# The shifted copies of the rotary embedding, issued on the ACT queue instead of the SP queue

## Chip, cores and metric

The kernel runs on one core of a Trainium2 chip. The metric is the device time of one execution in microseconds (us); lower is better. The engines are named as in the profile: PE does the matrix products, DVE, ACT and POOL work elementwise, and SP does no arithmetic: it issues DMA transfers. Each engine takes its instructions strictly in order, and so does each queue of DMA issues.

## What is computed

A two-layer encoder over 16 meta tokens and 512 tokens of width 2048. Layer 0 is attention with 16 query heads and 8 key heads of width 128; layer 1 is a gated linear attention. The change touches layer 0 alone, where every query and key head is normalised and rotated:

```python
def _rotate(x, ang):
    x1, x2 = jnp.split(x, 2, axis=-1)
    return jnp.concatenate([x1 * cos - x2 * sin, x2 * cos + x1 * sin], axis=-1)
...
q = apply_axial_rope(rmsnorm(q, q_norm), ang_row, ang_col)
k = apply_axial_rope(rmsnorm(k, k_norm), ang_row, ang_col)
...
p = softmax(q k^T / sqrt(128)); o = p v; y = (o * silu(gate)) @ w_out
```

A head is held with its 128 channels on the partitions and the 528 tokens along the free axis. The rotation mixes channels 0 to 31 with 32 to 63, and 64 to 95 with 96 to 127, so it needs a copy of the head in which these blocks of 32 partitions have changed places.

## The kernel before

Every float32 product is made of three matmuls on split operands (high by high, high by low, low by high): `uh` and `ul` are the normalised input, `whi` and `wlo` the weights. A unit of weights is 512 KB: SP loads it into `wraw` (two buffers, L151), ACT casts it to `whi` (L133), DVE takes the rest as `wlo` (L134), with three buffers of each.

Layer 0 runs over eight groups g of one key head and two query heads. While the attention of group g runs, `qkv(g + 1)` projects the next key head and the two next query heads, and `rope` rotates each: 24 rotations in all, three of them one right after the other at the start (group 0) and 21 spread over the groups. I call the three of a group K, Q1 and Q2. The steps of one rotation are these:

- ACT evacuates the two halves of the projection to `qw` (L293) and their squares to `sq` (L294);
- four DMAs, 32 partitions each, write the shifted copy `qs` from `qw` (L301); `qs` has one buffer;
- ACT and DVE split the squares into `sh` and `sl` (L133, L134), POOL multiplies `qw` by the cosines (L306, which overwrites what the four copies read) and `qs` by the sines (L307);
- PE sums the squares into `ssq` (L312, L313), DVE adds epsilon (L314), ACT makes the reciprocal root (L137, L138);
- DVE adds the two products (L316), multiplies by the root (L317), and ACT and DVE split the result into `qh`, `ql` or `kh`, `kl`.

Around them stand the steps of the attention: PE makes the scores `s` (L561 to L563), DVE their maximum `mx` (L566), ACT the exponentials `pn` (L569), DVE scales them (L570 to L572), PE transposes them to `pT` and, for the meta tokens, `pTm` (L579, L581), ACT copies these to `ph` and `pmt` (L583, L585), DVE takes the rests `pl` and the low part of `pmt` (L584, L586), and PE forms the output `o` (L599 to L602, ACT copies it at L603). `pT`, `pTm` and `ssq` share two PSUM buffers in turn, so a `pTm` can be written only when the last-but-one of these tiles has been read.

The code is written in one order, and the scheduler of the framework sets the order on each engine from priorities and its own estimate of durations. Weights have the higher priority: they are written to be issued up to 400 steps ahead.

Of the kernel before, what the change touches and what calls it, by code (L numbers as in the profile page):

```python
# [82 lines left out]
def hybrid_encoder(  # L83
# [5 lines left out]
    nc = tc.nc  # L89
# [42 lines left out]
    def split(hi, lo, src):  # L132
        A.copy(hi, src)  # L133
        V.tensor_tensor(lo, src, hi.bitcast(F32), op=ALU.subtract)  # L134

    def rsqrt_inplace(t):
        A.activation(t, t, AF.Ln)  # L137
        A.activation(t, t, AF.Exp, scale=-0.5)  # L138
# [158 lines left out]
    def rope(qw, sq, outs, ps_t):  # L297
        qs = wk.tile([P, T], F32, tag="qs", name="qs", bufs=1)
        for b in range(4):
            s = b ^ 1  # L300
            nc.sync.dma_start(out=qs[b * 32:b * 32 + 32, :], in_=qw[s * 32:s * 32 + 32, :])  # L301
        sh = wk.tile([P, T], F32R, tag="sh", name="sh", bufs=1)
        sl = wk.tile([P, T], F32R, tag="sl", name="sl", bufs=1)
        split(sh, sl, sq)
        f = sq
        G.tensor_tensor(qw, qw, cos, op=ALU.mult)  # L306
        G.tensor_tensor(qs, qs, sin, op=ALU.mult)  # L307

        def late():
            for a, b in HALVES:  # L310
                ps = ps_t.tile([P, 512], F32, tag="t", name="ssq")[:, :b - a]
                PE.matmul(ps, ones_r, sh[:, a:b], start=True, stop=False)  # L312
                PE.matmul(ps, ones_r, sl[:, a:b], start=False, stop=True)  # L313
                V.scalar_tensor_tensor(f[:, a:b], ps, 1.0 / P, erow[:, a:b], op0=ALU.mult, op1=ALU.add)  # L314
            rsqrt_inplace(f)
            V.tensor_tensor(qw, qw, qs, op=ALU.add)  # L316
            V.tensor_tensor(qw, qw, f, op=ALU.mult)  # L317
            for hi, lo, a, b in outs:
                split(hi, lo, qw[:, a:b])
        clk.after(3.7, late)  # L320
# [173 lines left out]
    for i in range(3):  # L494
        rope(*(taken(i) if i else head0), first_outs[i], ps_t)
        clk.flush()
# [44 lines left out]
    def qkv(g):  # L541
        qk, outs = qk_tiles()
        for i, c in enumerate((2048 + g * P, 2 * g * P, (2 * g + 1) * P)):
            qw, sq, evac = take(col(KN if i == 0 else QN))
            project(w_in0, c, HALVES, evac)
            rope(qw, sq, outs[i], ps_t)
        return qk, values(g)
# [811 lines left out]
```

## Time and profile before

| | |
|---|---|
| median of 3 runs | 1792.9 us (1791.56 to 1793.84) |
| the profiled execution | 1794.37 us, of which the span from first to last instruction is 1792.7 us |
| PE busy | 1766.4 us (99%) |
| DVE busy | 1036.8 us (58%) |
| ACT busy | 923.0 us (51%) |
| POOL busy | 199.1 us (11%) |
| the shifted copies | 96 DMAs of 66 KB, issued from 64.4 to 656.3 us |

The span is the time from the first to the last instruction. Issuing a DMA is not counted as busy time of an engine, but the queue of that engine stands while it lasts. In the rows of the profile an arrow `<-` behind a bracketed or listed time says how long the engine stood idle and whose result ended that.

### The profile page before, as it was taken

What the parts mean: (1) busy time and instruction counts of PE and PEld (TensorE: products, weight loads), DVE (VectorE), ACT (ScalarE), POOL (GpSimd) and SP (SyncE); (2) the same over time, 40 slices, a digit from 0 to 9 for tenths busy, and PEclk for the clock granted to TensorE, in tenths of its full rate; (3) what the DMA queues carried; (4) which work ended last, traced back from release to release, by engine and by line L of the source; (5) the groups of instructions that cost most, each with busy time, mean ns of one, the idle gap of its engine ahead of it and who ended that gap; (6) DMA issues with size and microseconds to landing.
All of it is one profiled execution on the core that took longest, in us unless ns stands there. A gap on an engine that the chain in (4) does not pass through costs nothing.

```text
span 1792.7 us, 31687 instructions
## 1 busy us (share of the span) xinstructions
PE 1766.4 (99%) x12711; PEld 1666.8 (93%) x12711; DVE 1036.8 (58%) x1807; ACT 923.0 (51%) x1875; POOL 199.1 (11%) x257
## 2 busy tenths in 40 slices
PE   8999999999999999999999999999999999999998
PEld 7899999999999999999999899988898989888886
DVE  4586555555656565632237887667685865764224
ACT  5665544454545454533238544477685765853221
POOL 3211111111111111111111101110000000000000
PEclk9999999999999999999999999999999999999999
DMA  8322232323232333343336444343242333344333
GB/s 260 119 61 83 84 89 84 89 83 90 83 89 82 91 105 94 121 131 91 96 92 205 120 128 132 93 135 96 83 113 82 103 95 88 92 151 176 94 95 129
DMA packets 263876, 193.93 MB, mean 108 GB/s; under 512 B 9356, under 2 KB 239440, under 8 KB 263200
## 3 DMA queue, kind: packets, MB, share of 16 engines
q1 hardware_dynamic: 254624, 162.52, 31.6%
q0 software_dynamic: 9104, 29.38, 4.7%
q8 instruction: 100, 1.64, 0.4%
q14 instruction: 48, 0.39, 0.1%
HBM read 160.88 MB, written 24.49 MB: 103 GB/s over the span
## 4 chain that ended last, share of the span: by engine, by line
PE 86%; DVE 5%; issue 3%; DMA 3%; ACT 2%; POOL 1%; SPq 0%; DVEq 0%; POOLq 0%; ACTq 0%
PE pp L156 18%; PE pp L158 18%; PE pp L157 18%; PE f L1271 2%; PE f L1269 2%; PE f L1270 2%; PE pp L233 2%; PE pp L235 2%; PE pp L234 2%; PE pT L579 2%; DMA wraw<-in_attn_w_in_dram 1%; PE s L561 1%; PE s L562 1%; PE s L563 1%; DVE wlo L134 1%
## 5 line engine op out<-in xcount | busy, mean ns | idle before, releaser
L156 PE MATMUL pp<-uh,whi 128*128 128x264 f32 (+1 forms) x2640 | 803.4, 304 | 0.8 <-ACT sq L294 0.4
L157 PE MATMUL pp<-ul,whi 128*128 128x264 f32 (+1 forms) x2640 | 793.9, 301 | 2.5 <-DVE ul L421 2.5
L158 PE MATMUL pp<-uh,wlo 128*128 128x264 f32 (+1 forms) x2640 | 794.0, 301 | 0.4 <-POOL wlo L360 0.3
L158 PEld LDWEIGHTS pp<-uh,wlo 128*128 128x128 f32 x2640 | 498.0, 189 | 17.5 <-POOL wlo L360 0.6
L156 PEld LDWEIGHTS pp<-uh,whi 128*128 128x128 f32 x2640 | 497.6, 189 | 17.4 <-ACT sq L294 0.5
L157 PEld LDWEIGHTS pp<-ul,whi 128*128 128x128 f32 x2640 | 498.2, 189 | 16.6 <-DVE ul L421 3.1
L134 DVE TENSOR_TENSOR wlo<-wraw,whi 128x1024 fp32r<-128x1024 f32 (+1 forms) x245 | 298.5, 1219 | 336.3 <-ACT whi L133 334.7
L133 ACT CAST whi<-wraw 128x1024 fp32r<-128x1024 f32 (+1 forms) x245 | 255.1, 1042 | 360.0 <-PE pp L157 197.5
L569 ACT ACTIVATE pn<-s,mx 128x528 f32<-128x528 f32 (+1 forms) x72 | 50.4, 700 | 105.6 <-DVE mx L566 105.5
L1271 PE MATMUL f<-whi,ul 128*128 128x512 f32 x192 | 75.6, 394 | 0.0
L1269 PE MATMUL f<-whi,uh 128*128 128x512 f32 x192 | 75.5, 393 | 0.0
L1270 PE MATMUL f<-wlo,uh 128*128 128x512 f32 x192 | 75.3, 392 | 0.0
L306 POOL TENSOR_TENSOR qw<-qw,cos 128x528 f32<-128x528 f32 x24 | 31.8, 1325 | 372.7 <-DMA qs<-qw 268.3
L566 DVE TENSOR_REDUCE mx<-s 128x1 f32<-128x528 f32 (+1 forms) x72 | 50.7, 704 | 31.2 <-PE s L563 29.8
L233 PE MATMUL pp<-th,whi 128*128 128x264 f32 x192 | 56.1, 292 | 1.1 <-ACT th L133 1.1
L584 DVE TENSOR_TENSOR pl<-pT,ph 128x512 fp32r<-128x512 f32 (+1 forms) x80 | 47.3, 591 | 13.9 <-ACT ph L583 12.9
L234 PE MATMUL pp<-tl,whi 128*128 128x264 f32 x192 | 54.5, 285 | 0.0
L316 DVE TENSOR_TENSOR qw<-qw,qs 128x528 f32<-128x528 f32 x24 | 17.0, 707 | 64.7 <-POOL qs L307 64.7
L235 PE MATMUL pp<-th,wlo 128*128 128x264 f32 x192 | 54.3, 284 | 0.0
L583 ACT CAST ph<-pT 128x512 fp32r<-128x512 f32 (+1 forms) x80 | 40.6, 508 | 15.3 <-DVE pl L584 7.8
L555 POOL TENSOR_TENSOR gs<-gs,gr 128x528 f32<-128x528 f32 x16 | 21.1, 1320 | 212.0 <-ACT gs L143 212.0
L133 ACT CAST whi<-x 128x1024 fp32r<-128x1024 f32 x27 | 28.1, 1043 | 30.8 <-PE pp L234 21.9
(381 smaller groups left out, 3305.3 us busy)
## 6 DMA issues: line engine op xcount, KB each, us to landing
wraw<-in_attn_w_in_dram SPq DMA_DIRECT2D x94, 512.0 KB, 4.0
wraw<-in_gla_w_in_dram SPq DMA_DIRECT2D x81, 512.0 KB, 3.9
wraw<-in_attn_w_out_dram SPq DMA_DIRECT2D x32, 512.0 KB, 3.9
wraw<-in_gla_w_out_dram SPq DMA_DIRECT2D x32, 512.0 KB, 3.8
x<-in_gla_w_in_dram SPq DMA_DIRECT2D x15, 512.0 KB, 4.6
qs<-qw SPq DMA_DIRECT2D x96, 66.0 KB, 3.2
x<-h_d SPq DMA_DIRECT2D x32, 132.0 KB, 3.9
h_d<-h POOLq DMA_DIRECT2D x16, 256.0 KB, 3.0
```

The lines of the kernel that those rows point to most:

```text
L133: A.copy(hi, src)
L134: V.tensor_tensor(lo, src, hi.bitcast(F32), op=ALU.subtract)
L156: PE.matmul(ps, wh, uh[:, k, a:b], start=first, stop=False)
L157: PE.matmul(ps, wh, ul[:, k, a:b], start=False, stop=False)
L158: PE.matmul(ps, wl, uh[:, k, a:b], start=False, stop=last)
L233: PE.matmul(ps, w[0][:, k], bh[:, k], start=k == 0, stop=False)
L234: PE.matmul(ps, w[0][:, k], bl[:, k], start=False, stop=False)
L235: PE.matmul(ps, w[1][:, k], bh[:, k], start=False, stop=k == KH - 1)
L566: V.reduce_max(mx, s, axis=AX.XY, negate=True)
L1269: PE.matmul(ps, uh[:, k, ts], wh[:, kk], start=(k == 0), stop=False)
L1270: PE.matmul(ps, uh[:, k, ts], wl[:, kk], start=False, stop=False)
L1271: PE.matmul(ps, ul[:, k, ts], wh[:, kk], start=False, stop=(k == KT - 1))
```

## The change

The four copies of a rotation are issued by ACT instead of SP. Data, buffers and every computing instruction stay the same.

```diff
@@ rope
         for b in range(4):
             s = b ^ 1
-            nc.sync.dma_start(out=qs[b * 32:b * 32 + 32, :], in_=qw[s * 32:s * 32 + 32, :])
+            nc.scalar.dma_start(out=qs[b * 32:b * 32 + 32, :], in_=qw[s * 32:s * 32 + 32, :])
         sh = wk.tile([P, T], F32R, tag="sh", name="sh", bufs=1)
```

SP keeps only loads of weights in this stage (80 in a row). On ACT the 96 issues are new, and the scheduler has moved instructions of PE, DVE and ACT around them. POOL's order is unchanged. Three places matter below.

ACT at the start, around the second rotation of group 0 (`qw_767`, `qs_773`, `sh_778`; the first rotation ends in `kh_703`), before:

```order
L138 ACTIVATE sq_708<-sq_708 128x528
L520 COPY vt_862<-pp_875 128x264
L133 CAST whi_990<-wraw_989 128x1024
L133 CAST kh_703<-qw_707 128x528
L294 ACTIVATE sq_768<-pp_148 128x264
L294 ACTIVATE sq_768<-g3_149 128x264
L133 CAST sh_778<-sq_768 128x528
L293 ACTIVATE qw_798<-g4_150,cols_87 128x264
```

and after:

```order
L138 ACTIVATE sq_708<-sq_708 128x528
L301 DMA qs_773<-qw_767 32x528
L133 CAST whi_990<-wraw_989 128x1024
L133 CAST kh_703<-qw_707 128x528
L294 ACTIVATE sq_768<-pp_148 128x264
L294 ACTIVATE sq_768<-g3_149 128x264
L301 DMA qs_773<-qw_767 32x528
L133 CAST whi_1210<-wraw_1209 128x1024
L301 DMA qs_773<-qw_767 32x528 x2
L133 CAST sh_778<-sq_768 128x528
```

The first of the four issues, which waits until the one `qs` buffer is free, now stands ahead of a cast of weights and of `kh`, and all four stand ahead of `sh_778`. On PE the matmuls that wait for `sh_778` have moved back by 28 places.

DVE in a rotation Q1 (here that of group 2: `qw_2072`, `qs_2320`), before:

```order
L572 TENSOR_SCALAR pn1_851<-pn1_851,sm_2392 128x3x16
L584 TENSOR_TENSOR pl_2248<-pT_2427,ph_2247 128x4x128
L586 TENSOR_TENSOR pmt_2249<-pTm_2432,pmt_2249 16x128
L316 TENSOR_TENSOR qw_2072<-qw_2072,qs_2320 128x528
L566 TENSOR_REDUCE mx_2463<-s_2456 128x1
L317 TENSOR_TENSOR qw_2072<-qw_2072,sq_2073 128x528
```

and after:

```order
L572 TENSOR_SCALAR pn1_851<-pn1_851,sm_2392 128x3x16
L314 SCALAR_TENSOR_TENSOR sq_2073<-ssq_2404,erow_97 128x264
L314 SCALAR_TENSOR_TENSOR sq_2073<-ssq_2408,erow_97 128x264
L316 TENSOR_TENSOR qw_2072<-qw_2072,qs_2320 128x528
L566 TENSOR_REDUCE mx_2463<-s_2456 128x1
L584 TENSOR_TENSOR pl_2248<-pT_2427,ph_2247 128x4x128
L317 TENSOR_TENSOR qw_2072<-qw_2072,sq_2073 128x528
L586 TENSOR_TENSOR pmt_2249<-pTm_2432,pmt_2249 16x128
```

The two reads of `pT_2427` and `pTm_2432`, which free the PSUM buffers of the next transposes, now stand behind the addition L316, which waits for the shifted copies. This exchange is found in all seven groups that have a Q1 rotation beside an attention.

ACT in the same rotation, after (before, the same rows without the issues, and `ph` ahead of `sh`):

```order
L294 ACTIVATE sq_2073<-pp_2205 128x264
L301 DMA qs_2320<-qw_2072 32x528 x4
L133 CAST sh_2325<-sq_2073 128x528
L583 CAST ph_2247<-pT_2358 128x4x128
L585 CAST pmt_2249<-pTm_2363 80x128
L569 ACTIVATE pn1_851,sm_2392<-s_2384,mx_2391 128x528
```

The four issues stand between the evacuation and the next exponential. PE's next transposes of this place, `pT_2485` and `pTm_2490`, keep their places in PE's order (the second moves back by one).

## The prediction

> **What bounds the kernel now.** The page comes first: the span and the engines' busy time.
>
> ```profile
> span 1792.7 us, 31687 instructions
> PE 1766.4 (99%) x12711; PEld 1666.8 (93%) x12711; DVE 1036.8 (58%) x1807; ACT 923.0 (51%) x1875; POOL 199.1 (11%) x257
> ```
>
> PE stands idle for 26.3 us in all. The busy time of stretches (length, then PE, PEld, DVE, ACT, POOL, each with its count) says where, in the part that has rotations:
>
> ```profile
> 50.00:100.00 50.00, 45.38 (x351) 44.08 (x350) 31.89 (x58) 31.56 (x69) 11.73 (x14) 0.97 0.37 108
> 200.00:300.00 100.00, 100.00 (x828) 99.72 (x827) 56.00 (x107) 48.77 (x104) 11.94 (x11) 1.00 0.32 91
> 300.00:650.00 350.00, 349.30 (x2889) 347.96 (x2888) 199.25 (x384) 170.39 (x361) 46.19 (x40) 1.00 0.29 85
> ```
>
> From 200 to 650 us PE is never free for a whole microsecond, at 0.121 us a matmul (100 us by 828). The three rotations of group 0 lie in the first stretch. The waits of PE from 60 to 660 us (total, times, longest):
>
> ```profile
> PE s L561 <- ACT sq L294: 1.1, 1, 1.1
> PE ssq L312 <- ACT sh L133: 0.9, 1, 0.9
> PE pT L579 <- DVE vm L536: 0.8, 1, 0.8
> ...
> PE pT L579 <- DVE sq L314: 0.4, 1, 0.4
> ```
>
> All of these lie before 101 us, and none is a wait for weights. So a queue that is relieved has nothing to give from 101 us on, and the change can win these 3.2 us at most. It can lose wherever it makes PE wait.
>
> **SP, which is relieved: 0.** The waits of SP's queue in the same stretch, and the issues:
>
> ```profile
> SPq L301 <- ACT qw L293: 61.6, 21, 5.0
> ...
> SPq L301 <- DVE qw L316: 7.9, 2, 4.0
> qs<-qw SPq DMA_DIRECT2D x96, 66.0 KB, 3.2
> L301 SPq DMA_DIRECT2D qs<-qw x96: 507/584/1461, 64.4 to 656.3; - x96
> ```
>
> 69.5 us of SP's waiting go away, and loads of weights that stood behind it go out earlier. PE waits for none of them, so I count nothing. If this cover were wrong, it would be a gain, inside the 3.2 us.
>
> **ACT, which is charged.** An issue takes 0.58 us of its queue (middle number above). A rotation K shows the four together, and what they delay:
>
> ```profile
> 257.25 0.39 ACT L294 ACTIVATE sq<-pp 128x264 f32<-128x264 f32 x1
> 257.42 2.41 SPq L301 DMA_DIRECT2D qs<-qw  x4
> 261.47 1.32 POOL L306 TENSOR_TENSOR qw<-qw,cos 128x528 f32<-128x528 f32 x1 [15.91 <-DMA qs<-qw]
> 262.55 0.69 ACT L569 ACTIVATE pn<-s,mx 32x528 f32<-32x528 f32 x1 [2.54 <-DVE mx L566]
> ```
>
> Four issues take 2.41 us; 24 rotations make 57.8 us of ACT's queue. No row shows an issue on ACT; I take SP's price, and the longest on SP (1.46) as the upper bound. In K the 2.41 us fit into the 2.54 us for which ACT waits before the exponential: 0 on the path. Were the cover gone (four at 1.46 are 5.84), the exponential would be 3.3 us late. The copies land 1.64 us after the last issue (257.42 + 2.41 = 259.83, to 261.47), from the same moment on either queue. The sums of squares `ssq` and their reciprocal root come later, but are placed 5 matmuls later in PE's order, and `kh` is for the next group: 0. In Q2 PE's order puts `ssq` 18 matmuls later (2.2 us, about the issues' time): 0.
>
> **Q1, the first term.** Here a load of weights went out between the copies. SP, ACT, POOL, DVE and PE in group 3:
>
> ```profile
> 276.52 0.51 SPq L301 DMA_DIRECT2D qs<-qw  x1
> 277.12 1.62 SPq L151 DMA_DIRECT2D wraw<-in_attn_w_in_dram  x1
> 278.80 1.85 SPq L301 DMA_DIRECT2D qs<-qw  x3
> 276.35 0.39 ACT L294 ACTIVATE sq<-pp 128x264 f32<-128x264 f32 x1
> 283.81 1.33 POOL L306 TENSOR_TENSOR qw<-qw,cos 128x528 f32<-128x528 f32 x1 [19.72 <-DMA qs<-qw]
> 285.11 1.31 POOL L307 TENSOR_TENSOR qs<-qs,sin 128x528 f32<-128x528 f32 x1
> 282.73 0.69 DVE L584 TENSOR_TENSOR pl<-pT,ph 128x512 fp32r<-128x512 f32 x1 [1.18 <-ACT ph L583]
> 283.45 0.29 DVE L586 TENSOR_TENSOR pmt<-pTm,pmt 16x128 fp32r<-16x128 f32 x1
> 286.45 0.71 DVE L316 TENSOR_TENSOR qw<-qw,qs 128x528 f32<-128x528 f32 x1 [2.71 <-POOL qs L307]
> 287.19 0.71 DVE L566 TENSOR_REDUCE mx<-s 128x1 f32<-128x528 f32 x1
> 287.82 0.70 DVE L317 TENSOR_TENSOR qw<-qw,sq 128x528 f32<-128x528 f32 x1
> 284.16 0.29 PE L563 MATMUL s<-kl,qh 128*128 128x264 f32 x1
> 286.56 0.27 PE L581 MATMUL pTm<-ident,pn 128*80 128x128 f32 x1
> ```
>
> Before, L584 and L586 freed the PSUM buffers at 283.74, long ahead of the transposes at 286.12 and 286.56, and the long wait for the copies (2.71 us before L316) cost nothing. Now L584 and L586 stand behind L316, so PE is tied to the landing of the copies.
>
> With t the time from the last issue to L306, L316 ends at 276.74 (end of `sq`) + 2.41 + t + 1.33 + 1.31 + 0.71 = 282.50 + t. The maximum L566 cannot start before the scores end (284.16 + 0.29 = 284.45). Behind it come L566 0.71, L584 0.69, L317 0.70 and L586 0.29, together 2.39. PE's `pTm` stands at 286.56 + 0.12 for the one place. So PE waits for 284.45 + 2.39 - 286.68 = 0.16 us if t is under 1.95, and one microsecond more for each above. K gives t = 1.64; here before it was 283.81 - 280.65 = 3.16, which gives 1.37 us. I take t = 2.25: the copies no longer stand behind the load in one queue, as in K, but the load runs at the same time. That is 0.16 + 0.30 = 0.46 us for each of seven groups: **3.2 us**, bounds 1.1 and 9.6. ACT's exponential of this place comes under 1 us late, and the scores that need its buffer (about 283.2) have 1.5 us of room.
>
> **The start, the second term.** Three rotations share one `qs`, so the first issue of the next waits for L316 of the one before, and ACT with it.
>
> ```profile
> 73.79 0.71 DVE L316 TENSOR_TENSOR qw<-qw,qs 128x528 f32<-128x528 f32 x1 [6.18 <-POOL qs L307]
> 76.58 0.63 ACT L133 CAST sh<-sq 128x528 fp32r<-128x528 f32 x1
> 77.00 0.63 SPq L301 DMA_DIRECT2D qs<-qw  x1
> 77.26 0.51 PE L312 MATMUL ssq<-sh,ones_r 128*128 128x264 f32 x2 [0.85 <-ACT sh L133]
> 81.20 1.32 POOL L306 TENSOR_TENSOR qw<-qw,cos 128x528 f32<-128x528 f32 x1 [7.44 <-ACT sq L137]
> 84.59 2.41 SPq L301 DMA_DIRECT2D qs<-qw  x4
> 86.35 0.39 PE L561 MATMUL s<-kh,qh 128*128 128x264 f32 x1 [1.10 <-ACT sq L294]
> 88.58 1.34 POOL L306 TENSOR_TENSOR qw<-qw,cos 128x528 f32<-128x528 f32 x1 [4.80 <-DMA qs<-qw]
> 91.50 0.71 DVE L316 TENSOR_TENSOR qw<-qw,qs 128x528 f32<-128x528 f32 x1
> ```
>
> Rotation two: from 74.50 ACT does an issue (0.60), a cast of weights (about 1.05), `kh` (0.63), two squares (0.77), an issue, a cast, two issues and `sh`: 74.50 + 4 x 0.60 + 2 x 1.05 + 0.63 + 0.77 = 80.4, then `sh` to 81.0 instead of 77.2. That is 3.8 us later, and PE has 28 matmuls (3.4 us) more ahead of the consumer: 0.4 lost. The copies land late by the same step: at K's 1.64 L306 starts at 82.0 instead of 81.2; at the 3.57 of this place (77.63 to 81.20), at 84.0. Rotation three: its last issue is about 2 us late (89.0, after 87.00), and so are L306 and L316. On DVE two L314, a rest of weights and a maximum now stand between L316 and L317, 2.1 us more. Against these 4.1 us stand 17 matmuls more ahead of the scores that need them (2.1 us) and about 0.8 us for which these scores' inputs lay ready: 1.3 us lost. The wait of 0.8 at `pT` may go in exchange, so I take half of it: **0.9 us**. Bounds: 1.9 gained (the waits of 1.1 and 0.8 both go), and 1.3 + 1.9 = 3.2 lost at the late landing.
>
> **Sum.** 3.2 + 0.9 = 4.1 us, bounds -0.8 and 12.8. The profiled execution took 1794.37 us, 1.5 above the median of 1792.9 (the span alone is 1792.7); against it the sum is 1798.5, against the median, which I predict for, **1797.0 us**. About 0.2% (3.6 us) is what a measurement of this kernel can tell from no change; the forecast lies just beyond, as a small loss.
>
> **Rivals.**
> - *No change that can be measured* (the other side). If t in Q1 is under 1.95 us, DVE waits for the scores and not for the copies: 1.1 us for seven groups. With a start of -1.9 to 1.9 this gives 1792.1 to 1795.9. For it: K lands in 1.64. Against it: in Q1 a load of 512 KB goes out at about the same moment. L306 starting before 281.1 in group 3 decides.
> - *The copies land no earlier than before*: t stays 3.16, so 9.6 us for Q1 and 3.2 for the start, 1805.7. For it: the only Q1 row; against it: K.
>   The Trainium skill, DMA: Bandwidth & Descriptors, section "Issuing engines are not separate DMA queues", says that transfers started by different engines run on the same 16 DMA engines and interleave, and that using several engines saves only the time to initiate, "usually small relative to the DMA itself". By its first half this rival holds; by its second the four issues would weigh nothing on ACT and the time would stay 1792.9. The trace disagrees on the second: four issues take 2.41 us, more than the 1.64 to the landing.
> - *An issue is dearer on ACT*: at 1.46 us, 3.4 us more for each rotation, less 0.1 of cover in K and nothing in Q1. Seven groups of 3.3 + 3.4 are 47 us, with the rest 1844. No row speaks for it but the longest issue.
> - *The relieved SP queue wins*: PE's waits at the start go, and Q1 costs nothing: 1792.9 - 3.2 = 1789.7. Against it: ACT's own chain becomes longer there.
>
> **Numbers.** Forecast 0.43 (1796 to 1801), no change 0.42, late landing 0.07, dearer issue 0.03, gain 0.05. Of the forecast's share about 0.03 lies under the bound of 0.2%. So slower 0.50, same 0.45, faster 0.05. The range leaves out the gain, the dearer issue and half of the late landing: 1792.3 to 1803.5.
>
> **What would show it.** In the profile after: ACT's queue with 96 issues of about 0.58 us; POOL's L306 of Q1 about 2.2 us behind the last issue; a new wait of PE, `pTm` or `pT` for DVE's L586 or L584, seven times about half a microsecond; at the start the waits at `ssq` and `s` near 81 and 87 us of a similar size, and one at the scores near 99 us. The forecast is wrong if PE shows no waits between 101 and 660 us, or if ACT's issues or the casts of weights behind them make PE wait elsewhere.

## The result, and the profile after

The changed kernel took 1806.7 us (median) beside 1793.5 us of the kernel before on the same chip: 1.0074 times as long, 95% interval 1.0060 to 1.0088, so 13.2 us slower. The forecast was a loss of 4.1 us, to 1797.0, with a range up to 1803.5. The direction came out; the size did not. One execution of the changed kernel took 6137 us at the full granted clock; the ratio leaves it out, and what held it up is not on record.

The head of the page of the changed kernel, its new DMA queue, and the median time of the copies from issue to landing (last number, us):

```profile
span 1805.8 us, 31656 instructions
PE 1772.9 (98%) x12711; PEld 1669.5 (92%) x12711; DVE 1040.3 (58%) x1807; ACT 921.9 (51%) x1875; POOL 199.8 (11%) x257
...
q10 hardware_dynamic: 4608, 6.49, 1.4%
...
qs<-qw ACTq DMA_DIRECT2D x96, 66.0 KB, 3.8
```

The issues by their line (shortest, median and longest in ns, first and last):

```profile
L301 ACTq DMA_DIRECT2D qs<-qw x96: 514/612/1730, 62.3 to 668.3; - x96
```

PE is idle for 32.9 us instead of 26.3, and busy for 6.5 us more with the same 12711 matmuls. The 96 issues cost 0.61 us each, close to the 0.58 taken; but the median time to the landing rose from 3.2 to 3.8 us, where the prediction let the landing in Q1 come earlier (t from 3.16 to 2.25) and the one in K stay.

The stretches shown of before, now of after, and then the waits of PE from 60 to 660 us (total, times, longest):

```profile
50.00:100.00 50.00, 45.70 (x354) 44.34 (x353) 31.09 (x55) 30.02 (x64) 12.52 (x14) 0.97 0.40 113
200.00:300.00 100.00, 98.36 (x807) 97.19 (x807) 56.53 (x109) 48.84 (x105) 11.61 (x10) 1.00 0.29 83
300.00:650.00 350.00, 346.44 (x2855) 343.94 (x2854) 195.84 (x371) 166.55 (x353) 43.89 (x38) 1.00 0.29 85
```

```profile
PE pT L579 <- DVE pl L584: 5.8, 5, 1.8
PE pT L579 <- DVE sq L314: 1.7, 3, 0.6
...
PE ssq L313 <- DVE sl L134: 1.5, 1, 1.5
...
PE pTm L581 <- DVE pmt L586: 0.5, 1, 0.5
```

The first stretch, the start, is as it was (45.70 busy, 45.38 before). The loss lies after it, where PE used to run without a gap: 21 matmuls fewer in 200 to 300 us, 34 fewer in 300 to 650. The waits are at the place forecast, `pT` and `pTm` for L584 and L586; those for L314 were not (two of the three are new, in Q1 of groups 2 and 6; the third ends at 109.67, and stood at 107.33 before).

How much each rotation costs is read from the matmul L602, which ends each of the four outputs `o` of a group. Before, then after, in group 3 on both sides of Q1:

```profile
271.23 0.29 PE L602 MATMUL o<-pmt,vm 80*128 80x256 f32 x1
288.55 0.29 PE L602 MATMUL o<-pmt,vm 80*128 80x272 f32 x1
```

```profile
277.31 0.28 PE L602 MATMUL o<-pmt,vm 80*128 80x256 f32 x1
296.15 0.29 PE L602 MATMUL o<-pmt,vm 80*128 80x272 f32 x1
```

The changed kernel enters this Q1 6.08 us late and leaves it 7.60 us late: it costs 1.52 us. In the same way the Q1 of groups 1 to 7 cost 2.36, 0.95, 1.52, 2.18, 1.18, 0.98 and 1.04: **10.2 us** of the 12.7 by which the last L602 is late. The rest is K of groups 2 and 3 (1.4) and the start with group 1. Q2 costs 0.4 in all.

What happens inside: Q1 of group 3 in the changed kernel, ACT and SP first, then POOL, DVE and PE (start, duration, engine, line):

```profile
282.43 0.39 ACT L294 ACTIVATE sq<-pp 128x264 f32<-128x264 f32 x1
282.62 2.94 ACTq L301 DMA_DIRECT2D qs<-qw  x4
282.77 13.67 SPq L151 DMA_DIRECT2D wraw<-in_attn_w_in_dram  x2
285.60 0.63 ACT L133 CAST sh<-sq 128x528 fp32r<-128x528 f32 x1 [2.77 <-issue]
286.77 0.70 ACT L569 ACTIVATE pn<-s,mx 128x528 f32<-128x528 f32 x1
288.71 1.31 POOL L306 TENSOR_TENSOR qw<-qw,cos 128x528 f32<-128x528 f32 x1 [16.50 <-DMA qs<-qw]
291.34 0.71 DVE L316 TENSOR_TENSOR qw<-qw,qs 128x528 f32<-128x528 f32 x1 [1.76 <-POOL qs L307]
291.96 0.70 DVE L566 TENSOR_REDUCE mx<-s 128x1 f32<-128x528 f32 x1
292.58 0.68 DVE L584 TENSOR_TENSOR pl<-pT,ph 128x512 fp32r<-128x512 f32 x1
293.91 0.29 DVE L586 TENSOR_TENSOR pmt<-pTm,pmt 16x128 fp32r<-16x128 f32 x1
293.41 0.63 PE L579 MATMUL pT<-ident,pn 128*128 128x128 f32 x4 [0.92 <-DVE pl L584]
294.25 0.31 PE L581 MATMUL pTm<-ident,pn 128*80 128x128 f32 x1
```

The first load of weights now goes out with the first copy (282.77 beside 282.62); before, it went out between the copies, and t was 3.16. The last issue ends at 285.56, and L306 starts 3.15 us later. L316 waits for the copies with L566, L584 and L586 behind it, and PE waits for L584. Over groups 1 to 7 the landing time t of Q1 was 4.32, 2.89, 3.15, 4.19, 3.23, 2.94 and 3.10 us: 3.4 on average, where 2.25 was taken. K shows why the 1.64 seen before was no property of the copies. Group 3, after:

```profile
262.66 2.50 ACTq L301 DMA_DIRECT2D qs<-qw  x4
262.81 0.37 SPq L151 DMA_DIRECT2D wraw<-in_attn_w_in_dram  x1
269.61 1.32 POOL L306 TENSOR_TENSOR qw<-qw,cos 128x528 f32<-128x528 f32 x1 [18.80 <-DMA qs<-qw]
```

t is 4.45 us here. In the K of groups 4 to 7 it is 2.92 to 3.09 us, and was 1.61 to 1.66 before. On SP the load had stood behind K's copies in the same queue (in group 3 it was issued at 259.93, right behind the last of them); relieved of them, it goes out beside them.

One thing more followed a wait. In group 1 PE stood for 1.82 us before `pT`, and then its clock fell to half (windows of the changed kernel; the third number from the right is the granted clock, 1.00 is full speed):

```profile
131.00 0.63 PE L579 MATMUL pT<-ident,pn 128*128 128x128 f32 x4 [1.82 <-DVE pl L584]
```

```profile
132.00:135.00 3.00, 3.00 (x16) 3.00 (x16) 2.95 (x5) 1.47 (x5) 0.00 (x0) 0.54 0.06 17
136.00:141.00 5.00, 5.00 (x44) 5.00 (x43) 1.23 (x1) 1.71 (x3) 0.00 (x0) 1.00 0.20 55
```

Sixteen matmuls in 3 us instead of 26 (44 in 5 us in the second row): more than 1 us lost while PE counts as busy. The kernel before has one such stretch between 60 and 660 us, at 62.54; the changed one has two, at 81.02 and 132.22.

### The profile page after: what moved, and what is told of

It reads as the page before. It is cut to its first block, busy times and chain, and to the rows that moved or that the text cites. A ratio compares the mean times of both kernels' runs of the same rounds, so it can differ in the third digit from the quotient of the medians.

```text
span 1805.8 us, 31656 instructions
## 1 busy us (share of the span) xinstructions
PE 1772.9 (98%) x12711; PEld 1669.5 (92%) x12711; DVE 1040.3 (58%) x1807; ACT 921.9 (51%) x1875; POOL 199.8 (11%) x257
## 3 DMA queue, kind: packets, MB, share of 16 engines
q8 instruction: 100, 1.64, 0.4%
## 5 line engine op out<-in xcount | busy, mean ns | idle before, releaser
L306 POOL TENSOR_TENSOR qw<-qw,cos 128x528 f32<-128x528 f32 x24 | 32.3, 1348 | 381.7 <-DMA qs<-qw 266.8
L566 DVE TENSOR_REDUCE mx<-s 128x1 f32<-128x528 f32 (+1 forms) x72 | 50.6, 703 | 28.0 <-PE s L563 27.4
L584 DVE TENSOR_TENSOR pl<-pT,ph 128x512 fp32r<-128x512 f32 (+1 forms) x80 | 47.2, 591 | 5.1 <-ACT ph L583 3.8
L579 PE MATMUL pT<-ident,pn 128*128 128x128 f32 (+1 forms) x288 | 42.2, 269 | 7.6 <-DVE pl L584 5.8
L583 ACT CAST ph<-pT 128x512 fp32r<-128x512 f32 (+1 forms) x80 | 40.6, 508 | 13.2 <-DVE pl L584 7.8
```

Source lines behind the costliest of these rows:

```text
L566: V.reduce_max(mx, s, axis=AX.XY, negate=True)
```

## The experiments

The leading theory ("tie"): Q1 pays, because L584 and L586 stand behind L316 on DVE and L316 waits for copies that land late beside a load. The main rival ("ACT"): the 57.8 us of issues on ACT's queue cost, wherever they stand. Differences to the kernel before are from runs on the same chip, where it took 1792.5 us. Each diff is against the kernel before or, for the tie cut, the loads taken away and L316 later, the changed kernel; `...`, `<...>` and the comments stand for code that is not shown.

**Q1 alone, and all but Q1.** The queue becomes an argument:

```diff
-    def rope(qw, sq, outs, ps_t):
+    def rope(qw, sq, outs, ps_t, queue=nc.sync):
-            nc.sync.dma_start(out=qs[...], in_=qw[...])
+            queue.dma_start(out=qs[...], in_=qw[...])
     # first: groups 1 to 7
+            rope(qw, sq, outs[i], ps_t, nc.scalar if i == 1 else nc.sync)
     # second: groups 1 to 7, and nc.scalar for the start
+            rope(qw, sq, outs[i], ps_t, nc.sync if i == 1 else nc.scalar)
```

> Only the copies of Q1 in groups 1 to 7 are issued on ACT; those of K and Q2 and the three of the start stay on SP. DVE's order in Q1 is that of the changed kernel (L584 and L586 behind L316). Theory 'tie' (the loss arises in Q1, because these two subtractions stand behind an addition that waits for late copies): about 10 of the 13 us stay, so 1801 to 1805 us. Rival 'ACT' (the 57.8 us of issues on ACT's queue are what costs, wherever they stand): 28 of 96 issues move, so about 4 of the 13 us, 1796 to 1798.

1803.0 us, ratio 1.0056 (1.0044 to 1.0068): 10.5 us slower with 28 of 96 issues moved.

> The opposite half: K and Q2 of groups 1 to 7 and the three rotations of the start are issued on ACT, Q1 of groups 1 to 7 on SP; DVE's order in Q1 is that of the kernel before. Theory 'tie': no waits of PE at pT or pTm in Q1; the start's 1 to 2.5 us and at most 1 us of K remain, so 1794 to 1798. Rival 'ACT': 68 of 96 issues move, about 9 us, so 1801 to 1804.

1793.3 us, ratio 1.0003 (0.9995 to 1.0012): no measurable difference with the other 68 moved (2.2 us at most, by the interval). The waits of PE from 60 to 660 us, with Q1 alone on ACT:

```profile
PE pT L579 <- DVE pl L584: 4.9, 5, 1.5
...
PE pT L579 <- DVE sq L314: 1.4, 3, 0.6
```

and with all but Q1 on ACT, where the row for L584 is gone:

```profile
PE o L599 <- ACT ph L583: 1.0, 2, 0.7
PE pT L579 <- DVE sq L314: 0.5, 1, 0.5
```

Most of the loss belongs to Q1. Time on ACT's queue as such costs nothing that these runs can tell, where "ACT" asked for 9 us: it falls.

**The tie cut, copies as late as ever.**

```diff
+        def last():   # 1 us later in the plan than the sums of squares
+            hold and V.scalar_tensor_tensor(qs[64:65, :1], <end of pmt>, 0.0, qs[64:65, :1], op0=ALU.mult, op1=ALU.add)
             V.tensor_tensor(qw, qw, qs, op=ALU.add)
```

> All copies on ACT as in the changed kernel. In Q1 of groups 1 to 7 an operation on one element, which reads the end of pmt and adds nothing to qs, stands ahead of L316, and L316 and L317 are written later, so that on DVE the maximum L566, L584 and L586 come ahead of L316. Issues, copies, loads and the places in PE's order stay. Theory 'tie': the waits of PE at pT and pTm in Q1 go although the copies land as late as before (about 5.2 to 6.5 us after the squares); 7 to 10 of the 13 us come back, 1796 to 1800, and the half-clock stretch at 132 us goes too. Rival 'ACT': issues stay, so 1805 to 1808.

1796.9 us, ratio 1.0021 (1.0012 to 1.0030): 4.3 us slower instead of 13.2. The waits of PE:

```profile
PE pT L579 <- DVE sq L314: 4.0, 5, 1.8
```

The waits for L584 are gone, with the issues and the loads where they were, and its trace shows no half-clock stretch at 132 us. Cutting the tie at L316 gave back 8.9 of the 13.2 us; by L602, 6.6 of them lie in the seven Q1, and 3.5 of these in group 1, where the half-clock stretch went too. What stayed is a second tie, at L314; it was longest in group 3, where L571 and L572, which stand ahead of L314, took 1.26 and 1.28 us.

**The loads taken away, the tie left.**

```diff
-            raw = wpool.tile([P, 1024], F32, tag="wraw", name="wraw", bufs=2)
+            raw = res[0] if res else wpool.tile(...)   # one resident tile from group 2 on
-            queue.dma_start(out=raw..., in_=src)
+            if not res: queue.dma_start(out=raw..., in_=src)
```

> As the changed kernel, but from group 2 on the projections of the first layer don't load their weights: every one splits one resident tile (so the result is not the reference's, and some 45 MB of loads are left out). DVE's order in Q1 is that of the changed kernel, ties included. Theory 'the load beside the copies makes them late': L306 starts about 1.6 us after the last issue in K, Q1 and Q2 of groups 2 to 7, as in the stretches without a load at the start (1.57), and PE's waits at pT and pTm in these six Q1 fall from about 1.2 us to 0.3 or less: 5 to 8 us less than the changed kernel, 1798 to 1802. Rival 'ACT's own queue lands later' or 'ACT's issues cost': L306 stays about 3 us behind the last issue, and the time stays 1805 to 1808.

1803.8 us, ratio 1.0060 (1.0048 to 1.0072): only 1.9 us better than the changed kernel, and the two intervals overlap. Half of the expectation came true. In groups 2 to 7 L306 starts 1.56 to 1.72 us after the last issue in 16 of 18 rotations (the others 2.46 and 3.28): the load beside the copies was what made them late, and ACT's queue is no slower to land. But each of these six Q1 still costs 1.0 to 1.9 us. The waits, and Q1 of group 3:

```profile
PE pT L579 <- DVE sq L314: 5.6, 7, 1.5
```

```profile
284.58 1.32 POOL L306 TENSOR_TENSOR qw<-qw,cos 128x528 f32<-128x528 f32 x1 [15.07 <-DMA qs<-qw]
285.87 1.50 POOL L307 TENSOR_TENSOR qs<-qs,sin 128x528 f32<-128x528 f32 x1
286.11 1.30 DVE L572 TENSOR_SCALAR pn<-pn,sm 128x48 f32<-128x48 f32 x1
287.45 0.77 DVE L314 SCALAR_TENSOR_TENSOR sq<-ssq,erow 128x264 f32<-128x264 f32 x2
287.94 0.66 PE L579 MATMUL pT<-ident,pn 128*128 128x128 f32 x4 [0.96 <-DVE sq L314]
288.14 0.70 DVE L316 TENSOR_TENSOR qw<-qw,qs 128x528 f32<-128x528 f32 x1
```

L316 waits for nothing now. But the transposes need the PSUM buffers that the sums of squares held, and L314, which frees them, stands behind the softmax's L570 to L572; in the kernel before it stood ahead of them. These are late. In group 3 `sh` starts on ACT only at 283.01, behind the four issues, and from `sl` (283.68), which waits for it, to the end of L314 (288.22) DVE works with no gap over 0.04 us through L584, L586 and L570 to L572. The exponential is not what it waits for: that was done at 284.98, and L570 started at 285.34, right behind L586. And as the copies come early, POOL's L307 runs beside L572, which takes 1.30 us instead of 0.25, in six Q1 out of six. In all ten traces up to 670 us, the 24 L572 that took 1.28 to 1.35 us started while L306 or L307 was running on POOL, and each ended 0.05 us behind it; six that started up to 0.18 us ahead of such a product took 0.25. The Trainium skill, SBUF — State Buffer, section "SBUF: two separate sides", says that GpSimd and some VectorE instructions share one pair of ports as an exclusive lock, which the one that starts first holds for its whole instruction. These ends and starts agree with that. Taking the late landing away thus gave most of its gain to the second tie.

**Both ties cut: the issues give way.**

```diff
-            nc.sync.dma_start(out=qs[...], in_=qw[...])
+            with tc.high_priority(-give_way): nc.scalar.dma_start(out=qs[...], in_=qw[...])
+            rope(qw, sq, outs[i], ps_t, 30 if i == 1 else 0)
```

> All copies on ACT as in the changed kernel, but in Q1 of groups 1 to 7 their issue gives way to work of ACT that is ready: ph, sh and pmt come first, then the four issues, then the exponential. With that the order of PE in Q1 is that of the kernel before, and on DVE L314 stands ahead of L570 to L572, and L584 and L586 ahead of L316. The copies go out some 1.5 us later than in the changed kernel and land beside the loads as late as there. Theory 'place in the order' (the loss is two ties on DVE: the transposes wait for L314 behind L570 to L572, which stand behind a late exponential, and for L584 and L586 behind L316): both ties are gone, 1793 to 1796 us, no wait of PE at pT or pTm in the seven Q1. Rival 'late copies or issues cost in any order': 1800 us or more.

1795.0 us, ratio 1.0016 (1.0007 to 1.0025): 2.5 us slower. Q1 of group 3:

```profile
282.60 0.77 DVE L314 SCALAR_TENSOR_TENSOR sq<-ssq,erow 128x264 f32<-128x264 f32 x2 [0.27 <-PE ssq L313]
284.59 1.34 POOL L306 TENSOR_TENSOR qw<-qw,cos 128x528 f32<-128x528 f32 x1 [15.89 <-DMA qs<-qw]
285.71 0.29 DVE L586 TENSOR_TENSOR pmt<-pTm,pmt 16x128 fp32r<-16x128 f32 x1
287.25 0.71 DVE L316 TENSOR_TENSOR qw<-qw,qs 128x528 f32<-128x528 f32 x1 [1.25 <-POOL qs L307]
288.69 0.60 PE L579 MATMUL pT<-ident,pn 128*128 128x128 f32 x4
```

The copies land 2.3 to 3.4 us after the last issue in these Q1, L316 waits for them, and PE does not: seven Q1 cost 0.0 us together. By L602, 1.2 us of what is left arise ahead of group 1's Q1, and 0.9 in K of groups 2 and 3.

**The same tie with an early landing, on SP.** From group 1 on, the four copies of a rotation stand together and ahead of the loads:

```diff
-            nc.sync.dma_start(out=qs[...], in_=qw[...])
+            with tc.high_priority(ahead): nc.sync.dma_start(out=qs[...], in_=qw[...])
+            rope(qw, sq, outs[i], ps_t, 1000)
```

> All copies on SP as in the kernel before, but from group 1 on the four copies of a rotation stand together in SP's queue, ahead of the loads of weights that stood between or ahead of them. On DVE in Q1, L584 and L586 stand behind L316, L314 ahead of L570. No issue on ACT. Theory: the copies land about 1.6 us after the last issue in Q1 and Q2 also, so L316 ends about 7.4 us after the squares, some 2 us ahead of the transposes that need L584 and L586: the same tie costs nothing, 1791 to 1794 us. POOL's products then run beside L571 and L572, which may become slow (1.3 us instead of 0.25 in the kernel without loads); this fits into the same 2 us. Rival 'the tie alone costs': about 1 us for each Q1, 1799 to 1801.

1792.1 us, ratio 1.0000 (0.9992 to 1.0009). Five of seven Q1 land in 1.60 to 1.64 us and cost 0.07 us at most, though L584 and L586 stand behind L316 and L572 takes 1.31 us in four of them: L314 is ahead of it. In group 1 the copies landed after 3.00 us, and it cost 0.36. In group 4 they landed 3.64 us after the last issue, and there the tie shows:

```profile
366.61 2.41 SPq L301 DMA_DIRECT2D qs<-qw  x4
372.66 1.32 POOL L306 TENSOR_TENSOR qw<-qw,cos 128x528 f32<-128x528 f32 x1 [18.49 <-DMA qs<-qw]
375.30 0.71 DVE L316 TENSOR_TENSOR qw<-qw,qs 128x528 f32<-128x528 f32 x1 [3.67 <-POOL qs L307]
376.66 0.66 PE L579 MATMUL pT<-ident,pn 128*128 128x128 f32 x4 [0.34 <-DVE pl L584]
377.60 0.31 PE L581 MATMUL pTm<-ident,pn 128*80 128x128 f32 x1 [0.28 <-DVE pmt L586]
```

This Q1 costs 1.05 us, on SP and without one issue on ACT. So the tie at L316 costs by the landing time, and the queue is only one way to set it.

**L316 made later still.**

```diff
+        [G.tensor_copy(*(((pad_t, qs), (qs, pad_t))[j % 2])) for j in range(pad)]   # pad = 2 in Q1
         G.tensor_tensor(qs, qs, sin, op=ALU.mult)
```

> The changed kernel with two more copies on POOL between L306 and L307 in Q1 of groups 1 to 7 (qs to a spare tile and back, values unchanged). A cast of 128x512 took POOL 0.61 us at the start, so L307, and L316 behind it, come about 1.26 us later in seven places. DVE's and PE's orders in Q1 are those of the changed kernel. Theory 'PE is tied to the end of L316': one for one, 7 x 1.26 = 8.8 us over the changed kernel, 1813 to 1817 us. Rival 'the wait at L314 and the late exponential carry the loss and L316 has room': 1806 to 1810.

1816.2 us, ratio 1.0131 (1.0117 to 1.0145): 23.6 us slower than the kernel before, 10.4 more than the changed kernel. The seven Q1 cost 18.8 us by their L602 instead of 10.2. The waits of PE:

```profile
PE pT L579 <- DVE pl L584: 9.9, 6, 2.9
```

Measured from the first issue, L316 ended 8.4 us later in the sum of the seven, and they cost 8.6 more. One for one: PE is tied to the end of L316. A 2.90 us wait in group 1 was followed by the half-clock stretch at 132 us again.

**The start alone.** Only the three rotations of group 0 get `nc.scalar`.

> Only the three rotations of the start are issued on ACT, all others on SP as before. Theory (the start's term as predicted): 0.9 us over the kernel before, between 1.9 less and 3.2 more; the kernel with K, Q2 and the start on ACT, at 0.7 us over, speaks for the low end: 1791.5 to 1794.5. Rival 'the copies of the start are held up behind ACT's casts and cost 2 to 3 us': 1795 to 1796.

1792.3 us, ratio 0.9995 (0.9986 to 1.0004): no difference.

| Q1, cost in us (L602) | 1 | 2 | 3 | 4 | 5 | 6 | 7 | sum |
|---|---|---|---|---|---|---|---|---|
| changed kernel | 2.36 | 0.95 | 1.52 | 2.18 | 1.18 | 0.98 | 1.04 | 10.2 |
| Q1 alone on ACT | 1.92 | 1.01 | 1.56 | 1.82 | 1.05 | 1.14 | 0.89 | 9.4 |
| tie at L316 cut | -1.15 | 0.82 | 2.51 | -0.02 | 0.74 | 0.80 | -0.06 | 3.6 |
| no loads from group 2 | 0.62 | 1.03 | 1.29 | 1.90 | 0.99 | 1.03 | 1.01 | 7.9 |
| issues give way | -0.02 | 0.00 | 0.01 | 0.03 | -0.05 | 0.02 | -0.04 | 0.0 |
| copies first, on SP | 0.36 | 0.00 | 0.07 | 1.05 | 0.00 | 0.00 | 0.01 | 1.5 |
| L316 later | 3.70 | 2.30 | 2.66 | 3.09 | 2.50 | 2.30 | 2.23 | 18.8 |

No version here is measurably faster than the kernel before: its PE waits for nothing that these queues could give, as the prediction's first part said.

## Why the prediction was wrong

- **SP relieved: 0.** Right for PE's waits. But the step asked only who waits for the loads, not beside what they would run once they are free. That is what made K's copies late and kept those of Q1 late. "All of these lie before 101 us" misreads the view: the 0.4 ended at 107.33, and rows not shown there hold 1.4 us before L487 at 60.76 and 0.7 before L525 at 398.16, so 3.2 us was not all that could be won. No version won any of it.
- **ACT charged.** The price was right: 2.41 taken for four issues, 2.44 to 2.50 measured mostly (2.94 in group 3's Q1). "0 on the path" held for Q2 (0.4 in all). K cost 1.4 us in groups 2 and 3 and nothing from group 4 on.
- **The Q1 term is the step that failed, by its t.** "I take t = 2.25" rested on K's 1.64, said to be the same "from the same moment on either queue". K's 1.64 was a landing without a load beside it, and the change took that away: t measured 3.4 on average. With it, group by group, the prediction's own formula, 0.16 + (t - 1.95), gives 2.53, 1.10, 1.36, 2.40, 1.44, 1.15 and 1.31, 11.3 us in all; measured were 10.2, each group within 0.3. The mechanism (L584 and L586 behind L316) was right, and the kernel with L316 later shows it one for one. In groups 2 and 6 the closeness is partly luck: there L572 took 1.31 and 1.35 us, and PE's wait at `pT` ended with L314, which the formula does not have.
- **The same term overlooked L314.** On ACT it asked about the exponential, "under 1 us late", and the scores that need its buffer. It did not ask about `sh`, which waits behind the issues too (2.77 us in group 3), nor about L314, which in the new order of DVE stands behind what follows `sh`: `sl`, L584, L586 and L570 to L572. L314 frees the transposes' buffers. So "0.16 us if t is under 1.95" was wrong on ACT: with t at 1.6 the kernel without loads still lost about 1 us in each Q1. The rival "no change" rested on that sentence and falls with it.
- **The start: 0.9.** Its bounds held, but not by its working: the start alone gave 0.9995 (0.9986 to 1.0004), -0.2 us where 0.9 was taken. The sum 74.50 + ... = 80.4 put the issues of the second rotation and ACT's casts one after another, `sh` done at 81.0 and L306 at 82.0. In the changed kernel the issues ran beside the casts that stood ahead of them (two issues from 75.19 to 76.35 beside a cast from 74.97 to 76.02, the last beside `kh` and the squares): `sh` was done at 78.59 and L306 started at 78.55. An issue held up only what came behind it. Nor does the sum add up as written: 4.1 less 2.1 and 0.8 is 1.2, not 1.3, and the 0.4 of the second rotation is not in it.
- **The rivals.** "The copies land no earlier than before" came closest (t 3.16 and 1805.7; 3.4 and 1806.7). It was given little weight, since K spoke against it; yet K was the one rotation of a group whose copies had no load beside them, and in the trace before Q2 stood at 2.94 to 3.50 in all seven groups, as Q1 at 2.61 to 3.67. That it came within 1 us is partly luck: it put 9.6 us on Q1, where 10.2 were lost, but 3.2 on the start, where the start with group 1's K lost 0.7, and nothing on the K and Q2 that lost the rest. The Trainium skill, DMA: Bandwidth & Descriptors, section "Issuing engines are not separate DMA queues", says that transfers of two queues interleave on the same 16 DMA engines. The landings agree with it: 1.6 us without a load, 2.9 to 4.3 beside one.
- **What stays open.** Why t varies between 2.9 and 4.3 beside the same load; with Q1 on ACT beside its loads, groups 1 and 4 were the latest in every kernel. Why K of groups 2 and 3 cost 1.4 us and later ones nothing; without the loads these two cost 0.2, so the loads have a part in it. Neither was tried by itself. That the slow L572 is due to POOL is seen at each place (1.3 us behind a POOL product that runs, 0.25 without one), not tested by itself.

## What to carry to other kernels

When a transfer leaves a queue, ask what stood behind it there and will now run at the same time: a short landing time may be owed to the order of the queue. An instruction that waits for a transfer costs by what stands behind it on its engine, so read there who frees the buffers that the bound engine needs next. Here the order was what hurt: with the issues giving way the seven Q1 cost 0.0 us, while taking the loads away without touching the order left 7.9 of 10.2 us to the next tie. Leaving the copies on SP was still the faster version.

## What the runs showed of the hardware

- The half clock came in stretches of 3.413 us. The two of the changed kernel begin 51.2 us apart (81.02 and 132.22), which is 15 times 3.413, and in the 3.41 us just before them PE was idle for 2.17 and 1.92 us. The length of a wait alone does not decide: waits of 1.45 us (ending at 81.10) and 1.82 us went with a fall, one of 1.72 us at 385.57 did not, nor did waits of 2.56 and 2.08 us in the kernel with L316 later. If the 3.41 us steps are counted on from 132.22, one ends at 384.81 and divides the wait of 1.72 us into 0.96 and 0.76; that this is why no fall followed is inferred, not tested, and in the kernel with L316 later two steps with 1.6 us of idle time went one each way. The Trainium skill, TensorE: Matmul & The Clock Gate, section "Part 1: The HAM clock gate (the "warmup" mystery)", tells of a fall after an idle window of about 3.4 us. Here PE was idle for between half and two thirds of such a window, and the measurement decides.
- Busy time hides waits: of 13.1 us of span, PE's idle time shows 6.6, and the other 6.5 stand as longer busy time, some of it the half clock (one stretch more than before). The time between two marked matmuls tells more than the idle column.
